# Branch hints for the matmul engine, chunk order inside the branches, and an earlier place for two blocks, in a two-layer transformer kernel

## The chip, the cores and the metric

One core of one Trainium2 chip. The metric is the device time of one execution in microseconds (us), the median over several runs. TensorE (PE) does matmuls (PEld is its weight load), VectorE is DVE, ScalarE ACT, GpSimd POOL; SyncE (SP) issues the transfers. Each engine runs its own instruction stream, branches included, and meets the others at semaphores.

## The reference, cut to what matters

256 tokens of width 1024 pass a first block (mLSTM and sparse attention, then a mixture of experts) and a second block (attention and a state-space branch). The change lies in the mixture of experts: each token goes to 4 of 32 experts; the grouping by expert depends on the data.

```python
logits = xf @ w_router + b_router
vals, idx = lax.top_k(logits, TOP_K);  gate = softmax(vals)
...
up = xb @ w_up[eb] + b_up[eb]            # [1024 x 2048] per expert
glu, lin = split(up, 2);  glu = min(glu, 7);  lin = clip(lin, -7, 7)
act = glu * sigmoid(1.702 * glu) * (lin + 1)
y = act @ w_down[eb] + b_down[eb]        # [1024 x 1024] per expert
```

After it the sum over experts is normalised (with the weight row `g_post_ffn`) and added to the residual.

## The kernel before, in words

**Weights.** All weights come through one stream of 1 MB transfers on SP's queue (class `Stream`, L159 to L189). In the expert part it owns 15 buffers of 1 MB; an expert needs 12 (8 of `w_up`, 4 of `w_down`). `ws.done(n)` gives a buffer back and issues the next transfer, in the order of the calls; SP waits there until the last reader of that buffer has finished. So a late reader holds back not only its buffer's successor but every transfer behind it.

**Loop (L2150 to L2200).** Step e computes expert e's up product and then expert e-1's down product. Tokens of an expert are split in chunks of 32 slots. The first chunk is always computed: for every fourth expert the token gather (tile `pga`), the bias (`up_bias`), 8 k-steps of matmuls into `pU` (one per 1 MB buffer), `swiglu`; then `down` into `pY`, a transpose `paT`, and `scatter` into `yacc`. How many tokens an expert has is known only at run time: `rv[e]` is loaded into registers of PE, ACT and DVE at k = 3 of step e (L2174).

**Branches.** `over_up(e)` (L2111) runs under `tc.If(rv[e] > 32)`: the second chunk into `pUo` and, nested in a second `tc.If(rv[e] > 64)`, the gather (`pgo`) and up product of the third chunk. `over_down(e-1)` (L2118) does the same for the down product, after the step's `scatter`. The body of such a branch is straight code; if the condition is false the engine jumps over it to a short arm in which it raises the semaphores that the body would have raised (EVENT_SEMAPHORE rows). In this input 13 experts have over 32 tokens, and two of them (11 and 25) over 64. The second chunk reads the same 8 (or 4) weight buffers as the first, and they are released after `over_up` (or `over_down`).

**After the loop.** L2202 to L2204: `far`, chunks 4 to 8 of every expert, all under one `tc.If(cmax > 96)` that PE, ACT, DVE and SP evaluate; here it is false, and the engines jump over it. Its weights would go to slots 3 and 4 of the pool `AR`. Then the last norm: squares of `yacc` into `jk` (L2213), `yg`, the reciprocal root, the residual, and block 2. The norm's weight row `gg2` is made in the loop's extra step e = 32 by `row_of` (8 transposes `prow`, two evictions), just before `over_down(31)`.

Of the kernel before, what the change touches and what calls it, by code (L numbers as in the profile page):

```python
# [7 lines left out]
F32 = mybir.dt.float32  # L8
# [5 lines left out]
OP = mybir.AluOpType  # L14
# [3 lines left out]
ET = mybir.EngineType  # L18
EPS = 1e-6

S, D = 256, 1024
# [134 lines left out]
NE = 32  # L156
# [189 lines left out]
def build(tc, A, out):  # L346
    nc = tc.nc
# [105 lines left out]
    def par(n):  # L453
        return cut(n, (PK, PK0, pk) if n in PK else (PK1, 0, [None, part.get("pk1")]))
# [64 lines left out]
    modc = con.tile([128, 48], F32, name="modc")  # L519
# [38 lines left out]
    def row_of(out, col, tiles, back=None):  # L558

        for j0 in range(0, 8, 4):  # L560
            t = yield from tiles(f"prow{j0}")
            for j in range(4):
                PE.transpose(t[:, 128 * j:128 * j + 128], col[:, j0 + j:j0 + j + 1].to_broadcast([128, 128]), ident)
            yield
            ev(out[:, 128 * j0:128 * j0 + 512], t)
            if back:
                back(f"prow{j0}")

    def at_once(f):
        def g(name):  # L570
            return f(name)
            yield
        return g
# [771 lines left out]
    t = PY("pmod")  # L1345
# [471 lines left out]
    t = []  # L1817
# [138 lines left out]
    rv = {}  # L1956
# [24 lines left out]
    def gates_lane():  # L1981

        pr, sm = sb.tile([128, 2, 4], F32, name="pr"), sb.tile([128, 2, 2], F32, name="sm")
        V.tensor_scalar(sm[:, :, 0:1], mx[:, :, 0:1], -1.0, None, op0=OP.mult)
        for i in range(2):
            ACT.activation(pr[:, i], mx[:, i, 0:4], AF.Exp, bias=sm[:, i, 0:1], accum_out=sm[:, i, 1:2])
        V.reciprocal(sm[:, :, 1:2], sm[:, :, 1:2])
        V.tensor_tensor(pr, pr, sm[:, :, 1:2].to_broadcast([128, 2, 4]), op=OP.mult)
        V.tensor_tensor(hit, hit, pr[:, :, :, None].to_broadcast(wide), op=OP.mult)
        V.tensor_reduce(gates, hit.rearrange("p i j e -> p i e j"), axis=AX.X, op=OP.add)  # L1990

        V.tensor_scalar(ghalf, gates, 0.5, None, op0=OP.mult)
        yield
        tg = PM("pgT")
        for i in range(2):
            PE.transpose(tg[:32, 128 * i:128 * i + 128], gates[:, i], ident)
        ACT.copy(gT, tg[:32, :256])
        yield
        for i in range(2):
            for n in range(2):  # L2000
                PE.matmul(yacc[i][n], gT[:, 128 * i:128 * i + 128], bd[:, 512 * n:512 * n + 512], start=True, stop=False,
                          skip_group_check=True)
        yield

    def up_bias(e, U):
        for q in range(4):
            PE.matmul(U[32 * q:32 * q + 32], e96[:, e:e + 1].to_broadcast([96, 32]),
                      bu3.rearrange("p (b c) -> p b c", b=2)[:, :, 256 * q:256 * q + 256], start=True, stop=False,
                      skip_group_check=True)
# [36 lines left out]
    def down(aT, wd):  # L2046

        t = PM("pY")
        for k in range(8):
            h, c = divmod(k, 2)  # L2050
            for q in range(4):
                PE.matmul(t[32 * q:32 * q + 32, 0:256], aT[:, c, 32 * h:32 * h + 32],
                          wd[k // 2][:, k % 2, 256 * q:256 * q + 256], start=k == 0, stop=k == 7, skip_group_check=True)
        return t
# [6 lines left out]
    def y_out(t, y):  # L2061
        for q in range(4):
            o, c = 32 * q, 256 * (q % 2)
            (ACT.copy if q % 2 else V.tensor_copy)(y[o:o + 32, c:c + 256], t[o:o + 32, 0:256])  # L2064
# [29 lines left out]
    def chunk_up(e, x, wu, act):  # L2094
        U = PO("pUo")
        up_bias(e, U)
        for k in range(8):
            up_k(U, x(k), k, wu(k))
        lc, th = (sb.tile([128, 256], F32, name=n, tag=n) for n in ("lco", "tho"))
        swiglu(U, act, lc, th)  # L2100

    def chunk_down(e, b, act, wd):
        gl_ = slots(e, 32 * b, "Go")
        next(gl_)
        a = sb.tile([128, 2, 128], F32, name="aTo", tag="aTo")
        act_T(act, a)
        g = next(gl_)
        y_out(down(a, wd), yz[2])
        scatter(g, yz[2])

    def over_up(e, wu, xT):  # L2111
        with tc.If(rv[e] > 32):  # L2112
            chunk_up(e, lambda k: xT[:, e % 4, k, 32:64], wu, ov[:, 2 * (e % 2)])
            with tc.If(rv[e] > 64):
                x = gather_chunk(e, 2)
                chunk_up(e, lambda k: x[:, k], wu, ov[:, 2 * (e % 2) + 1])

    def over_down(e, wd):  # L2118
        with tc.If(rv[e] > 32):
            chunk_down(e, 1, ov[:, 2 * (e % 2)], wd)  # L2120
            with tc.If(rv[e] > 64):
                chunk_down(e, 2, ov[:, 2 * (e % 2) + 1], wd)

    def far(e, r, b=3):

        with tc.If(r > 32 * b):
            x = gather_chunk(e, b)

            def weights(src, k):
                t = AR(3 + k % 2, "wf", [128, 2048])  # L2130
                v = t.rearrange("p (a b) -> p a b", a=src[0])
                SP.dma_start(v, src[2])
                return v

            lu, ld = block_loads(A["w_up"][e], 0, 2048, 1), block_loads(A["w_down"][e], 0, 1024, 2)
            chunk_up(e, lambda k: x[:, k], lambda k: weights(lu[k], k), ov[:, 4])
            wf = {}

            class Late:
                def __getitem__(self, k):  # L2140
                    if k not in wf:
                        wf[k] = weights(ld[k], k)
                    return wf[k]
            chunk_down(e, b, ov[:, 4], Late())
            if b < 7:
                far(e, r, b + 1)

    aT = {}
    gl = gates_lane()
    for e in range(NE + 1):  # L2150
        if e < NE:
            i0 = at[f"up{e}"][0]
            steps = iter(())
            if e % 4 == 0:
                xT = AR(0, "xT", [128, 4, 8, 64])
                steps = gather(xT, e, min(4, NE - e))
                next(steps)
            U = PU("pU")
            up_bias(e, U)
            act, lc, th = (sb.tile([128, 256], F32, name=n, tag=n, bufs=b) for n, b in (("act", 2), ("lc", 1), ("th", 1)))  # L2160
            if e:
                gs = slots(e - 1, 0, "G", 2)
                next(gs)
            wu = lambda k: ws.get(i0 + k)
            for k in range(8):
                if k % 2 == 0:
                    next(steps, None)
                up_k(U, xT[:, e % 4, k, 0:32], k, wu(k))
                if e == 0 and k < 3:
                    next(gl)  # L2170
                if e and k == 2:
                    g = next(gs)
                if k == 3:
                    rv[e] = nc.values_load(counts[0:1, e:e + 1], engines=(ET.PE, ET.Activation, ET.DVE), min_val=0, max_val=256)  # L2174
            swiglu(U, act, lc, th)
            over_up(e, wu, xT)
            for j in range(8):
                ws.done(i0 + j)
        if e:
            d0 = at[f"down{e - 1}"][0]  # L2180
            wd = [ws.get(d0 + k) for k in range(4)]
            if e == NE:
                gs = slots(e - 1, 0, "G", 2)
                next(gs)
                g = next(gs)
                gg2, ggc = AR(0, "gg2", [128, D]), sb.tile([128, 8], F32, name="ggc2")
                V.tensor_tensor(ggc, modc[:, 40:48], par("g_post_ffn"), op=OP.mult)
                for _ in row_of(gg2, ggc, at_once(PM)):
                    pass
                over_down(e - 1, wd)  # L2190
            y_out(down(aT[e - 1], wd), yz[e % 2])
        if e < NE:
            aT[e] = sb.tile([128, 2, 128], F32, name="aT", tag="aT", bufs=2)
            act_T(act, aT[e])
        if e:
            scatter(g, yz[e % 2])
            if e < NE:
                over_down(e - 1, wd)
            for k in range(4):
                ws.done(d0 + k)  # L2200
    many = (ET.PE, ET.Activation, ET.DVE, ET.SP)
    with tc.If(nc.values_load(cmax[0:1, 0:1], engines=many, min_val=0, max_val=256) > 96):  # L2202
        for e in range(NE):
            far(e, nc.values_load(counts[0:1, e:e + 1], engines=many, min_val=0, max_val=256))  # L2204

    sq, ss, rs = (sb.tile([128, n], F32, name=f"{m}3") for m, n in (("sq", 4), ("ss", 2), ("rs", 2)))
    yg = AR(8, "yg", [128, 2, D])
    jk = AR(7, "jk", [128, D])
    s3 = con.tile([128, 2], F32, name="ss4")
    for n in (1, 0):  # L2210
        for i in range(2):
# [37 lines left out]
```

## Time and profile before

| | |
|---|---|
| median of 3 runs | 1713.04 us (1710.18 to 1717.36) |
| the profiled execution's own time | 1716.04 us |
| its span, first to last instruction | 1714.2 us |
| mean granted TensorE clock | 0.935 |
| PE busy | 1424.8 us, 83% |
| bytes moved | 526 MB, 403 MB of them expert weights |

The expert part spans 254 to 1274 us of it. Times in rows are us from the span's start. A row of a timeline reads: start, length, engine, line, operation, tiles (out<-in), shape, count, and in brackets the idle time before it with what ended it. "PEq L2112" is PE's sequencer at a branch of that line, "issue" an idle time for which the profile shows no wait. Most operations are recorded by one helper and bear its line, L145; tiles tell them apart.

### The profile page before, as it was taken

The page shows a single profiled execution, that of the slowest core. Times are in us where ns is not written, and L with a number is a line of the kernel's source. Part 1 is how long each engine was busy: PE and PEld are TensorE (multiplying, and loading weights), DVE is VectorE, ACT ScalarE, POOL GpSimd, SP SyncE. Part 2 cuts the span into 40 slices and gives each one's busy share as a digit, 9 for nine tenths or more (in the row PEclk, how much of TensorE's full clock was granted, in tenths as well). Part 3 has the DMA queues.
Part 4 walks back from the last instruction along what each step waited for, and adds up shares of the span by engine and source line. Part 5 has one row for each costly group of instructions (what it writes and reads, how often), then busy time and mean ns, then how long its engine had stood idle before and what let it go on. Part 6 is the DMA issues. An engine that isn't in the chain of part 4 may idle for free. (4 is left out here: it accounts for less than half of the span.)

```text
span 1714.2 us, 28511 instructions
## 1 busy us (share of the span) xinstructions
PE 1424.8 (83%) x11403; PEld 845.3 (49%) x11403; DVE 661.5 (39%) x1508; ACT 435.9 (25%) x980; POOL 271.9 (16%) x387
## 2 busy tenths in 40 slices
PE   5999988887798898777766778887858888999998
PEld 2775652332233243232132233333227788999996
DVE  3556462121121122121111111221136798766767
ACT  3545331010010011010010010010025555654553
POOL 1127100000000000000000000000005652552533
PEclk8999999999899999889788988999988999999999
DMA  9746896999999988999999998999924344333452
GB/s 377 285 157 219 314 369 267 423 420 422 421 418 420 414 322 353 420 423 421 422 421 421 413 414 336 387 367 420 420 81 148 99 146 144 130 99 113 162 177 91
DMA packets 116487, 526.03 MB, mean 307 GB/s; under 512 B 8744, under 2 KB 11216, under 8 KB 80304
## 3 DMA queue, kind: packets, MB, share of 16 engines
q1 hardware_dynamic: 113392, 518.67, 76.0%
q10 hardware_dynamic: 2496, 3.92, 0.7%
q8 instruction: 157, 2.57, 0.6%
q0 software_dynamic: 384, 0.39, 0.1%
q14 instruction: 58, 0.48, 0.1%
HBM read 521.50 MB, written 1.06 MB: 305 GB/s over the span
## 5 line engine op out<-in xcount | busy, mean ns | idle before, releaser
L145 PE MATMUL pU<-w,xT 128*32 128x512 f32 x2048 | 266.2, 643 | 29.7 <-DMA w<-in_w_up 22.3
L145 PE MATMUL pg<-h,wH 128*128 128x256 f32 x1296 | 249.4, 292 | 9.8 <-ACT wH L254 3.1
L145 DVE TENSOR_TENSOR wL<-w,wH 128x512 fp32r<-128x512 f32 (+2 forms) x244 | 174.2, 728 | 111.1 <-PE pg L145 59.4
L145 PEld LDWEIGHTS pg<-h,wH 128*128 128x128 f32 x1296 | 205.5, 195 | 23.3 <-issue 7.0
L145 PE MATMUL pY<-w,aT 128*32 128x256 f32 x2048 | 151.2, 445 | 73.1 <-PEq L2112 41.3
L254 ACT CAST wH<-w 128x512 fp32r<-128x512 f32 (+4 forms) x312 | 176.1, 587 | 116.0 <-PE pg L145 101.7
L145 PE MATMUL pg<-h,wL 128*128 128x256 f32 (+1 forms) x648 | 186.2, 287 | 6.3 <-DVE wL L145 3.7
L145 POOL TENSOR_TENSOR xt<-yg,xt 128x512 f32<-128x512 f32 x1 | 1.5, 1485 | 1025.9 <-ACT yg L2219 1025.9
L145 PEld LDWEIGHTS pY<-w,aT 128*32 128x32 f32 x2048 | 79.3, 125 | 157.2 <-issue 74.8
L145 PEld LDWEIGHTS pU<-w,xT 128*32 128x32 f32 x2048 | 62.7, 115 | 171.9 <-issue 114.8
L145 DVE COPY yz<-pY 32x256 f32<-32x256 f32 x94 | 39.2, 417 | 248.6 <-PE pY L145 227.6
L145 PEld LDWEIGHTS pg<-h,wL 128*128 128x128 f32 (+1 forms) x648 | 125.7, 194 | 8.0 <-DVE wL L145 4.8
L145 POOL TENSOR_TENSOR wL<-w,wH 128x512 fp32r<-128x512 f32 (+2 forms) x68 | 87.8, 1297 | 222.6 <-PE pg L145 135.7
L2064 ACT COPY yz<-pY 32x256 f32<-32x256 f32 x94 | 34.1, 363 | 304.4 <-DVE yz L145 304.4
L145 PE MATMUL yacc<-yz,G 64*128 64x512 f32 x256 | 91.9, 627 | 17.8 <-ACT yz L2064 17.8
L2021 ACT ACTIVATE th<-act 128x256 f32<-128x256 f32 x32 | 13.3, 416 | 357.8 <-DVE act L145 357.8
L145 PE MATMUL pUo<-w,xT 128*32 128x512 f32 x832 | 92.1, 595 | 0.0
L145 DVE COPY G<-pG 128x256 f32<-128x256 f32 x32 | 13.6, 424 | 183.9 <-PE pG L145 183.9
L145 DVE TENSOR_SCALAR act<-pU 128x256 f32<-128x256 f32 x32 | 13.6, 424 | 155.5 <-PE pU L145 155.5
L145 PE MATMUL pg<-wH,h 128*128 128x512 f32 (+2 forms) x224 | 69.4, 393 | 3.6 <-ACT wH L254 1.9
L145 PE MATMUL pg<-yk,wH 128*128 128x256 f32 x384 | 68.6, 281 | 0.1
L145 PE MATMUL pY<-w,aTo 128*32 128x256 f32 x960 | 54.9, 380 | 9.1 <-DVE Go L145 8.5
(451 smaller groups left out, 1950.1 us busy)
## 6 DMA issues: line engine op xcount, KB each, us to landing
w<-in_w_up SPq DMA_DIRECT2D x256, 1024.0 KB, 17.3
w<-in_w_down SPq DMA_DIRECT2D x128, 1024.0 KB, 19.7
w<-in_w_in SPq DMA_DIRECT2D x48, 1024.0 KB, 4.9
w<-in_w_ada SPq DMA_DIRECT2D x24, 1024.0 KB, 8.5
w<-in_ada_w SPq DMA_DIRECT2D x12, 1024.0 KB, 6.7
w<-in_w_out SPq DMA_DIRECT2D x8, 1024.0 KB, 4.9
w<-in_w_branch_ssm SPq DMA_DIRECT2D x8, 1024.0 KB, 4.9
w<-in_w_branch_att SPq DMA_DIRECT2D x4, 1024.0 KB, 4.9
```

The costliest lines, as they stand in the source:

```text
L145: return f(*a, **k)
L254: self.nc.scalar.copy(H[:, a:b], p)
L2021: ACT.activation(th, act, AF.Tanh, scale=0.5 * 1.702)
L2064: (ACT.copy if q % 2 else V.tensor_copy)(y[o:o + 32, c:c + 256], t[o:o + 32, 0:256])
```

## The change

Four edits, all in the expert part. (1) `announce` marks, for PE only, a hint for the coming branch `up{e}` or `down{e}`, with the condition in a register; the mark for `up{e}` stands right after `up_bias`, that for `down{e-1}` ahead of `down` of the same step (for the last expert ahead of its step's releases). So the count is loaded one expert earlier. (2) Inside both branches the third chunk's `If` now stands ahead of the second chunk. (3) The far block moves from behind the loop to the start of step 31; its weights use slot 7. (4) `gg2` is made there too, in slot 7, and `jk` takes slot 0.

```diff
+    def announce(what, e):
+        tc.mark_branch_hint_location(f"{what}{e}", hint=rv[e] > 32, engines=hints)
...
     def over_up(e, wu, xT):
-        with tc.If(rv[e] > 32):
-            chunk_up(e, lambda k: xT[:, e % 4, k, 32:64], wu, ov[:, 2 * (e % 2)])
+        with tc.If(rv[e] > 32, label=f"up{e}"):
             with tc.If(rv[e] > 64):
                 x = gather_chunk(e, 2)
                 chunk_up(e, lambda k: x[:, k], wu, ov[:, 2 * (e % 2) + 1])
+            chunk_up(e, lambda k: xT[:, e % 4, k, 32:64], wu, ov[:, 2 * (e % 2)])
...
     def over_down(e, wd):
-        with tc.If(rv[e] > 32):
-            chunk_down(e, 1, ov[:, 2 * (e % 2)], wd)
+        with tc.If(rv[e] > 32, label=f"down{e}"):
             with tc.If(rv[e] > 64):
                 chunk_down(e, 2, ov[:, 2 * (e % 2) + 1], wd)
+            chunk_down(e, 1, ov[:, 2 * (e % 2)], wd)
...
-                t = AR(3 + k % 2, "wf", [128, 2048])
+                t = AR(7, "wf", [128, 2048])
...
+    rv[0] = counted(0)
     for e in range(NE + 1):
+        if e == NE - 1:
+            many = (ET.PE, ET.Activation, ET.DVE, ET.SP)
+            with tc.If(nc.values_load(cmax[0:1, 0:1], engines=many, min_val=0, max_val=256) > 96):
+                for o in range(NE):
+                    far(o, nc.values_load(counts[0:1, o:o + 1], engines=many, min_val=0, max_val=256))
+            gg2, ggc = AR(7, "gg2", [128, D]), sb.tile([128, 8], F32, name="ggc2")
+            V.tensor_tensor(ggc, modc[:, 40:48], par("g_post_ffn"), op=OP.mult)
+            for _ in row_of(gg2, ggc, at_once(PM)):
+                pass
...
             up_bias(e, U)
+            announce("up", e)
...
-                if k == 3:
-                    rv[e] = nc.values_load(counts[0:1, e:e + 1], engines=(ET.PE, ET.Activation, ET.DVE), min_val=0, max_val=256)
+                if k == 3 and e < NE - 1:
+                    rv[e + 1] = counted(e + 1)
             swiglu(U, act, lc, th)
             over_up(e, wu, xT)
+            if e == NE - 1:
+                announce("down", e)
...
                 over_down(e - 1, wd)
+            else:
+                announce("down", e - 1)
             y_out(down(aT[e - 1], wd), yz[e % 2])
```

The old places of the far block and of `gg2` are removed, and `jk = AR(7, ...)` becomes `jk = AR(0, ...)`.

## Rows read from the trace of the kernel before

**Rows 1.** Windows: stretch, length, busy PE PEld DVE ACT POOL, clock, DMA share, GB/s.

```profile
269.00:280.00 11.00, 10.43 (x101) 3.07 (x94) 2.46 (x7) 1.09 (x3) 0.00 (x0) 1.00 0.01 1
280.00:588.00 308.00, 252.28 (x2272) 99.82 (x2276) 59.76 (x153) 27.92 (x70) 0.00 (x0) 0.93 1.01 418
1028.00:1114.00 86.00, 72.62 (x660) 29.86 (x656) 16.44 (x45) 7.99 (x21) 0.00 (x0) 0.92 0.89 363
1114.00:1226.00 112.00, 91.59 (x812) 36.69 (x807) 20.86 (x53) 9.83 (x24) 0.00 (x0) 0.94 0.98 399
```

**Rows 2.** Waits of SP's queue: us in total, times, longest us.

```profile
SPq L180 <- PEq L2112: 131.7, 19, 12.5
SPq L180 <- PEq L2114: 129.6, 11, 26.2
```

**Rows 3.** Lines L2112, L2119, L2121, PE's branches: ns min/median/max, first and last start.

```profile
L2112 PEldq COMPARE_BRANCH  x32: 70/434/5938, 270.0 to 1225.0; - x32
...
L2119 PEldq COMPARE_BRANCH  x32: 65/414/6402, 299.7 to 1252.3; - x32
...
L2121 PEldq COMPARE_BRANCH  x26: 70/190/1507, 309.6 to 1263.2; - x26
```

**Rows 4.** Waits of PE, branch of L2112: us in total, times, longest.

```profile
PE pY L145 <- PEq L2112: 41.3, 17, 5.2
```

**Rows 5.** Timeline, PE and SP, expert 0's second chunk.

```profile
272.31 7.05 PE L145 MATMUL pUo<-w,xT 128*32 128x512 f32 x64
...
279.52 0.33 SPq L180 DMA_DIRECT2D w<-in_w_up  x1
```

**Rows 6.** Timeline of PE, expert 11's third chunk.

```profile
600.45 5.05 PE L145 MATMUL pgo<-So,xh 128*128 128x32 f32 x32 [2.22 <-DVE So L145]
...
605.91 8.78 PE L145 MATMUL pUo<-w,xo 128*32 128x512 f32 x64
```

**Rows 7.** Timeline of SP and PE, expert 25; time to landing from the page.

```profile
1007.99 2.54 SPq L180 DMA_DIRECT2D w<-in_w_up  x5
...
w<-in_w_up SPq DMA_DIRECT2D x256, 1024.0 KB, 17.3
...
1021.53 0.62 PE L145 MATMUL pU<-bu,e 96*32 96x512 bf16 x4 [4.27 <-PEq L2119]
1021.91 4.70 PE L145 MATMUL pU<-w,xT 128*32 128x512 f32 x24
```

**Rows 8.** Windows, the same columns, expert 25's first matmuls.

```profile
1021.00:1026.00 5.00, 4.46 (x24) 1.25 (x28) 0.00 (x0) 0.00 (x0) 0.00 (x0) 0.52 1.01 415
```

**Rows 9.** Timeline of PE, experts 26 to 31.

```profile
1066.24 4.48 PE L145 MATMUL pU<-w,xT 128*32 128x512 f32 x24 [3.50 <-DMA w<-in_w_down]
...
1125.15 2.05 PE L145 MATMUL pga<-S,xh 128*128 128x256 f32 x8 [4.38 <-PEq L2119]
...
1170.44 4.92 PE L145 MATMUL pY<-w,aT 128*32 128x256 f32 x44 [5.12 <-PEq L2112]
...
1189.99 2.75 PE L145 MATMUL pU<-w,xT 128*32 128x512 f32 x24
...
1213.01 0.40 PE L145 MATMUL pU<-bu,e 96*32 96x512 bf16 x4
...
1225.02 1.07 PE L145 MATMUL pU<-w,xT 128*32 128x512 f32 x8 [1.57 <-DMA w<-in_w_up]
```

**Rows 10.** Line L2202, the far block's branch on PE.

```profile
L2202 PEldq COMPARE_BRANCH  x1: 3726/3726/3726, 1269.5 to 1269.5; - x1
```

**Rows 11.** Timeline of PE and ACT, step 32 and the norm's start.

```profile
1252.26 1.06 PE L145 MATMUL prow<-cst__67,ggc 128*128 128x128 f32 x8 [0.68 <-DVE ggc L145]
1253.55 0.44 PE L145 MATMUL paT<-cst__67,ov 128*128 128x128 f32 x2 [0.24 <-ACT gg L515]
...
1268.20 2.83 PE L145 MATMUL yacc<-yz,G 64*128 64x512 f32 x8 [0.97 <-ACT yz L2064]
...
1273.40 0.60 ACT L2213 ACTIVATE jk<-yacc 128x512 f32<-128x512 f32 x1 [4.40 <-PEq L2202]
```

More of the change, by code (lines that the diff above doesn't have):

```diff
@@ L2109, in chunk_down @@
         scatter(g, yz[2])
+    hints = (ET.PE,)
+    def announce(what, e):
+        tc.mark_branch_hint_location(f"{what}{e}", hint=rv[e] > 32, engines=hints)
     def over_up(e, wu, xT):
-        with tc.If(rv[e] > 32):
-            chunk_up(e, lambda k: xT[:, e % 4, k, 32:64], wu, ov[:, 2 * (e % 2)])
+        with tc.If(rv[e] > 32, label=f"up{e}"):
             with tc.If(rv[e] > 64):
@@ L2149, in build @@
     gl = gates_lane()
+    counted = lambda e: nc.values_load(counts[0:1, e:e + 1], engines=(ET.PE, ET.Activation, ET.DVE), min_val=0, max_val=256)
+    rv[0] = counted(0)
     for e in range(NE + 1):
+        if e == NE - 1:
[7 more added lines that the diff above has]
+                pass
         if e < NE:
@@ L2185, in build @@
                 g = next(gs)
[L2186 to L2189, printed above, removed]
                 over_down(e - 1, wd)
+            else:
+                announce("down", e - 1)
             y_out(down(aT[e - 1], wd), yz[e % 2])
@@ L2200, in build @@
                 ws.done(d0 + k)
[L2201 to L2204, printed above, removed]
     sq, ss, rs = (sb.tile([128, n], F32, name=f"{m}3") for m, n in (("sq", 4), ("ss", 2), ("rs", 2)))
     yg = AR(8, "yg", [128, 2, D])
-    jk = AR(7, "jk", [128, D])
+    jk = AR(0, "jk", [128, D])
     s3 = con.tile([128, 2], F32, name="ss4")
```

## The prediction

> **What bounds the kernel now.** I read the windows by stage first, then the waits of SP and PE, then the single lines and the timeline. In the expert part the bound is mostly the weight stream: from 280 to 588 us the transfers are busy all the time at 418 GB/s, while PE is busy 252 of 308 us [rows 1]. At that pace a 1 MB buffer takes 2.5 us. A shorter PE therefore gains only where the stream goes unfed. That is so at the start (share 0.01 from 269 to 280) and behind experts 11 and 25, which have a third chunk (0.89 from 1028 to 1114, against 0.98 after it) [rows 1]. SP, when it waits for a buffer, waits most for PE's arrival behind a branch: 131.7 us at L2112 and 129.6 us at L2114, 11 times [rows 2].
>
> Two different things hide in these rows. At L2114 it is bookkeeping: the inner branch stands last, so with no third chunk all 8 buffers come free only in its empty arm, after the whole second chunk. At L2112 and L2119 it is the jump itself. A branch that is entered costs PE 0.07 us; one that is jumped costs up to 5.9 and 6.4 us [rows 3], and PE's matmuls behind L2112 waited 41.3 us for it [rows 4]. The inner jump at L2121, over a shorter body, never took over 1.5 us [rows 3]. So the cost hangs on how far the jump goes: code that is not there yet has to be fetched.
>
> **Part 1, the order of the chunks.** Expert 0 shows what a second chunk costs the stream. Its matmuls run from 272.31 for 7.05 us, and the first transfer after them is issued at 279.52 [rows 5]. With the inner branch ahead, PE first makes that short jump (I take 0.5 us, an estimate between the median of 0.19 and the worst of 1.5 [rows 3]); the first buffer is then free after an eighth of 7.05 us, so at 273.7, and one more every 0.9 us, faster than transfers take them. The stream restarts 5.6 us earlier; I take **-5.0**. As the stream is busy without a break until 588, this arrives there whole. The other ten such experts gain the same on paper, but there the queue still holds several transfers, and early buffers are worth nothing.
>
> Experts 11 and 25 pay for it. Before, the chunk that releases the buffers was the third one, and PE's 2.22 us wait for DVE's mask stood behind the second [rows 6]. Now the gather comes straight after the first chunk, where DVE is still in `swiglu` (about 2.9 us, an estimate from those 2.22 and the branches ahead of it), then the gather's 5.05, the third chunk's 9.3 with its bias, about 1.0 until DVE has emptied the single `pUo` buffer, then 1.2 to the first release: 19.4 us after the first chunk. Before it was 7.3 + 2.2 + 5.05 + 0.5 + 1.7 (the first k-step at the pace of [rows 6]) = 16.7. So the first buffer comes **+2.7** later, and PE is busy **+1.8** longer. After expert 11 other gains (the down buffers of expert 10, released early; a jump at expert 12) cancel this; I take 0 there.
>
> **Part 2, the hints.** A jump's price is more than its idle time. [...] The last `w_up` buffer of expert 25 was issued by 1010.1 and landed some 17.3 us later [rows 7], at 1027.4, so its first chunk could have ended at 1028.3; it ended near 1031.3 (1021.91 + 4.70, then 40 matmuls at the pace of expert 30 and a small transpose). With the jump at 0.4 us: **-3.0** (bounds 0 and -6.2). The same jump at expert 26 (4.38 us, and slow gather matmuls behind it [rows 9]) gives about **-6** on PE's chain. The one at expert 29 (5.12) I count at 0: by then the stream is the later of the two (below); its bound is -4.6. The marks are two more register steps and a marker on PE's sequencer, 64 times in all. PE's sequencer runs ahead of its matmuls (L2112's branch is executed before the matmuls ahead of it are done), and the stream covers the rest: 0; without that cover at most 0.1 to 0.2 us each (the entered branch's 0.07 and the inner jump's 0.19 are the nearest rows), some 2 us from expert 25 on. The counts' loads only move by one step: 0.
>
> **Part 3, the far block and the norm's row.** At the end two things go. The row of `gg2` holds PE from 1251.58 to 1253.55: **-2.0** [rows 11]. The far jump makes ACT start the norm at 1273.40, although the last `scatter` ended at 1271.03 [rows 11]: **-2.2**, leaving 0.15 for the semaphore. In step 31 they come back: the jump 3.7 us [rows 10] (transfers were idle then; 6.1, as the long ones of [rows 3], is likelier under load), the row 2.0, and slow first matmuls 2.0: 7.7 to 10.1, I take 10. ACT and DVE jump too, beside PE, and SP, which has up to eight transfers queued. The cover: expert 31's first chunk ran from 1213.01 to 1226.1, 13.1 us against 7.7 for one that waits for nothing (bias 0.4, 64 matmuls at 2.75 per 24), since it waited for its weights (the last wait, 1.57 us [rows 9]). So 5.3 of the 10 are hidden: **+4.7**.
>
> **The sum.** On PE's chain: -5.0 - 3.0 + 1.8 - 6.0 = -12.2 by expert 28. On the stream: -5.0 - 3.0 + 2.7 = -5.3 at expert 25's first release. Of what it goes unfed later (11% of 86 us is 9.5, of which expert 25 itself about 6; 2% of 112 is 2.2 [rows 1]) I let 4 go, through earlier releases: -9.3. The later counts: -9.3 into step 31, + 4.7 = -4.6 at the end of its first chunk, from where PE bounds until the norm; - 2.0 - 2.2 gives -8.8. Block 2 only shifts. The profiled execution took 1716.04 us, so 1707.2; it lies 3.0 above the median of the runs, so against that median I forecast **1704.2**.
>
> **The rivals.** *The hints do nothing* (never taken up, or the fetch is still late). Then PE's chain has -5.0 + 1.8 = -3.2, the stream about -4.3; -3.2 + 4.7 - 4.2 = -2.7, 1710.3. For it: nothing in this trace shows a hint at work. Against: between mark and branch lie over 100 PE instructions, 7 us or more, and the longest jump is 6.4.
>
> *The hinted code pushes out the code that comes next*, and the kernel is slower. The trace has such stalls in straight code: at expert 26 PE stood 3.50 us within a chunk (the transfer it is put down to is no match: that chunk reads `w_up`), and the next 24 matmuls took 4.48 [rows 9]: 5.2 us in all. From expert 25 on six hinted jumps are taken (up and down of 26, 27, 29). PE's chain without them stands at -12.2 + 4.7 - 4.2 = -11.7, so it decides from the third stall on; with four, +9.1, 1722. Against it: the inner jumps, right behind an entered branch, find their code. [...]
>
> *More goes than I count*: expert 26's straight-code stall is gone because the code lies differently, and the far jump costs 3.7. Then the stream has -12, the far block +2.7, the end -4.2: -13.5, 1699.5.
>
> *The inner jump misses*, now that it comes early in the body. Six second chunks of experts 28 to 31 depend on it; two misses of 3 us take 6 back, 1710.
>
> **How the numbers follow.** Forecast 0.45 (half of it beyond 0.5%, as it lies on that line), hints without effect 0.20, more than counted 0.17, pushed-out code 0.10, inner misses 0.08. 0.5% of the median is 8.6 us, about what a measurement of this kernel can tell from no change: faster 0.41, same 0.47, slower 0.12. The range takes the bounds of expert 29's jump and of the far block below, and reaches up to where three stalls stand: 1692 to 1719.
>
> **What would show it.** PE's longest branch at L2112 and L2119 under 1 us (else the hints fail); expert 0's first reissue near 274; expert 25's first reissue 19 to 20 us after its first chunk; the far branch ahead of expert 31's matmuls with 6 to 10 us of PE idle; ACT's `jk` right behind the last `scatter`. New "issue" stalls of 2 to 4 us would make the forecast wrong upwards, a stream without gaps behind expert 25 downwards.

## The result, and the profile after: 1.1% slower

The changed kernel took a median of 1732.66 us (1730.75 to 1734.33, 4 runs) against 1712.4 for the kernel before beside it (1710.18 to 1717.36, 4 runs): a ratio of 1.011, 95% interval 1.0089 to 1.013. The forecast was 1704.2, faster or the same. The profiled execution took 1730.75 us, its span is 1729.0 (before 1714.2).

Windows of the changed kernel, with the columns of [rows 1]; the last stretch is new.

```profile
269.00:280.00 11.00, 9.02 (x84) 2.36 (x80) 1.61 (x4) 0.42 (x1) 0.00 (x0) 0.96 0.32 102
280.00:588.00 308.00, 255.96 (x2313) 94.30 (x2305) 62.18 (x160) 28.36 (x71) 0.00 (x0) 0.93 1.02 421
1028.00:1114.00 86.00, 72.02 (x672) 31.48 (x672) 15.84 (x44) 7.58 (x20) 0.00 (x0) 0.92 0.87 354
1211.00:1246.00 35.00, 15.17 (x86) 5.07 (x86) 2.16 (x7) 1.32 (x3) 0.00 (x0) 0.71 0.72 292
```

The start did fill (share 0.32 where it was 0.01 [rows 1]). Behind expert 25 nothing improved (0.87, before 0.89). The loss sits in the last line: from 1211 to 1246 us PE is busy 15.17 of 35 us, and the granted clock there is 0.71, so part of its work goes by at a lower clock, 0.55 from 1239.9 to 1243.0 (the last 40 matmuls of the chunk take 5.83 us; at the pace of expert 30 [rows 9] they would take 4.58). Expert 30's first chunk still ends at 1197.15 (before 1197.54); expert 31's ends at 1245.80 (before 1226.08, 19.7 earlier). The last norm starts 14.9 us later than before [rows 11], and the span is 14.8 longer. So the difference between these two executions arises in one step of the loop: step 31 loses 20.1 us, and 4.8 come back before the norm.

Timeline of that step, PE, DVE and ACT:

```profile
1210.84 2.83 PE L145 MATMUL yacc<-yz,G 64*128 64x512 f32 x8 [0.57 <-ACT yz L2064]
...
1221.26 1.94 PE L145 MATMUL prow<-cst__67,ggc 128*128 128x128 f32 x8 [7.58 <-PEq L2161]
...
1223.53 3.80 PE L145 MATMUL pU<-w,xT 128*32 128x512 f32 x24
...
1238.24 0.59 ACT L515 COPY gg<-prow 128x512 f32<-128x512 f32 x1 [26.21 <-SPq L2161]
1238.29 0.69 DVE L145 COPY gg<-prow 128x512 f32<-128x512 f32 x1 [20.45 <-SPq L2161]
1238.90 0.59 DVE L145 TENSOR_SCALAR gt<-cst__68,pos,ghalf 128x128 f32<-128x128 f32 x2
1239.35 0.38 PEld L145 LDWEIGHTS pG<-cst__67,gt 128*128 128x128 f32 x2 [12.93 <-ACT gg L515]
1239.38 0.66 PE L145 MATMUL pG<-cst__67,gt 128*128 128x128 f32 x2 [12.05 <-DVE gt L145]
...
1239.97 5.83 PE L145 MATMUL pU<-w,xT 128*32 128x512 f32 x40
```

Read it from below. PE's `pG` waits 12.05 us for DVE's `gt`; DVE stands ahead of `gt` in the eviction of the norm's row into `gg2`; and that eviction waits, as ACT's does, for SP's sequencer at the far block's branch (L2161). The row's matmuls were done at 1223.2, so the row lay 15 us in PSUM. The source view of that branch says what SP did (operation, count, duration in ns, first and last start):

```profile
L2161 SPq EVENT_SEMAPHORE  x9: 17/17/17, 1228.9 to 1238.1; - x9
L2161 DVEq EVENT_SEMAPHORE  x2: 21/21/21, 1217.4 to 1217.6; - x2
L2161 ACTq EVENT_SEMAPHORE  x2: 17/17/17, 1218.3 to 1218.4; - x2
L2161 PEldq EVENT_SEMAPHORE  x2: 51/51/51, 1220.8 to 1221.0; - x2
...
L2161 PEldq COMPARE_BRANCH  x1: 6451/6451/6451, 1214.3 to 1214.3; - x1
...
L2161 SPq COMPARE_BRANCH  x1: 50/50/50, 1223.8 to 1223.8; - x1
```

PE, DVE and ACT raise two semaphores each in the short arm and are through at 1221. SP has nine. It reaches the branch at 1223.8; its own jump takes 5.0 us, to 1228.9. The fifth to the eighth semaphore go at 1230.62, 1233.09, 1235.57 and 1238.05, each 0.01 to 0.02 us behind the landing of a transfer of the weight stream (1230.60, 1233.08, 1235.56, 1238.04), and the ninth goes right after. Eight of the nine are the semaphores that the stream's transfers raise in turn: in the arm SP waits for each of them and then raises it, in place of the far block's transfers. So SP goes through its empty arm no faster than the transfers it has already issued land. `gg2` lies in slot 7, the slot the change gave to the far block's weights, and in the trace both evictions of the row wait for these same eight semaphores. From 1217.75 to 1249.18, 31 us, SP issued no transfer either.

A second loss is spread over the whole expert part. The wait for DVE's inner branch (L2119) did not exist before:

```profile
L2119 DVEq EVENT_SEMAPHORE  x11: 21/21/21, 274.3 to 1247.8; - x11
...
  PE pUo L145: 22.3, 11
```

In all 11 experts with a second but no third chunk, PE's second chunk waits 2.0 us (22.3 in all) for DVE's empty inner arm. `pUo` is one PSUM buffer. With the third chunk's `If` ahead, that arm is what releases it, and DVE gets there only after the `swiglu` of the first chunk. Expert 0, and expert 28, where the chunk itself also went slower:

```profile
274.39 0.40 PE L145 MATMUL pUo<-bu,e 96*32 96x512 bf16 x4 [1.98 <-DVEq L2119]
274.62 7.04 PE L145 MATMUL pUo<-w,xT 128*32 128x512 f32 x64
...
1139.05 0.40 PE L145 MATMUL pUo<-bu,e 96*32 96x512 bf16 x4 [2.03 <-DVEq L2119]
1139.27 1.02 PE L145 MATMUL pUo<-w,xT 128*32 128x512 f32 x3
1140.71 8.11 PE L145 MATMUL pUo<-w,xT 128*32 128x512 f32 x59 [0.41 <-issue]
```

The granted clock was 1.00 in the 10 us ahead of this and is 0.84 in the 11 us from 1139. Over all second chunks the page's mean of one such matmul rose from 595 to 640 ns.

The jumps did get shorter. Branches of the two outer `If`s on PE, minimum, median and maximum in ns (before: [rows 3]):

```profile
L2118 PEldq COMPARE_BRANCH  x45: 77/191/4712, 269.4 to 1252.4; - x45
L2125 PEldq COMPARE_BRANCH  x45: 70/290/6245, 297.0 to 1279.7; - x45
```

Added over the 38 that are jumped, they take 74.4 us instead of 130.1, and 19 of them take under 0.5 us (10 before). Some still cost the full price. At the end, the first square of `yacc` follows the last `scatter` (1286.29, 2.83 long) at once, no longer a far jump:

```profile
1288.30 0.60 ACT L2227 ACTIVATE jk<-yacc 128x512 f32<-128x512 f32 x1 [1.21 <-PE yacc L145]
```

### The profile page after: what moved, and what is told of

Its sections match the earlier page's. It is cut to its first block, busy times and chain, and to the rows that moved or that the text cites. A ratio compares the mean times of both kernels' runs of the same rounds, so it can differ in the third digit from the quotient of the medians.

```text
span 1729.0 us, 28678 instructions
## 1 busy us (share of the span) xinstructions
PE 1431.3 (83%) x11403; PEld 831.5 (48%) x11403; DVE 662.2 (38%) x1508; ACT 436.0 (25%) x980; POOL 272.2 (16%) x387
## 5 line engine op out<-in xcount | busy, mean ns | idle before, releaser
L145 PE MATMUL pY<-w,aT 128*32 128x256 f32 x2048 | 140.7, 418 | 53.2 <-DMA w<-in_w_down 31.2
L145 PEld LDWEIGHTS pU<-w,xT 128*32 128x32 f32 x2048 | 57.7, 114 | 185.3 <-issue 100.1
L145 PEld LDWEIGHTS pY<-w,aT 128*32 128x32 f32 x2048 | 68.8, 117 | 137.7 <-DMA w<-in_w_down 42.6
L145 PE MATMUL yacc<-yz,G 64*128 64x512 f32 x256 | 98.2, 687 | 16.8 <-ACT yz L2064 16.8
L145 PE MATMUL pUo<-w,xT 128*32 128x512 f32 x832 | 101.7, 640 | 0.4 <-issue 0.4
L145 DVE TENSOR_SCALAR act<-pU 128x256 f32<-128x256 f32 x32 | 13.6, 425 | 180.8 <-PE pU L145 180.8
L145 DVE COPY G<-pG 128x256 f32<-128x256 f32 x32 | 13.6, 425 | 151.3 <-PE pG L145 151.3
## 6 DMA issues: line engine op xcount, KB each, us to landing
w<-in_w_down SPq DMA_DIRECT2D x128, 1024.0 KB, 19.7
```

Source lines behind the costliest of these rows:

```text
L145: return f(*a, **k)
```

## The experiments

Every ratio is against runs of the kernel before on the same chip in the same session. Its medians there were 1714.09 (experiments 1 to 4), 1715.16 (5 to 8) and 1713.68 (9 to 12).

### Experiments 1 to 4: which part of the change loses

**1.** The changed kernel with the far block and the row back at their old places.

```diff
-                t = AR(7, "wf", [128, 2048])
+                t = AR(3 + k % 2, "wf", [128, 2048])
...
-        if e == NE - 1:
-            many = (ET.PE, ET.Activation, ET.DVE, ET.SP)
...
-            gg2, ggc = AR(7, "gg2", [128, D]), sb.tile([128, 8], F32, name="ggc2")
...
                 g = next(gs)
+                gg2, ggc = AR(0, "gg2", [128, D]), sb.tile([128, 8], F32, name="ggc2")
...
+    many = (ET.PE, ET.Activation, ET.DVE, ET.SP)
+    with tc.If(nc.values_load(cmax[0:1, 0:1], engines=many, min_val=0, max_val=256) > 96):
...
-    jk = AR(0, "jk", [128, D])
+    jk = AR(7, "jk", [128, D])
```

> Hints and the new chunk order, with the far block and the norm's row back at their old places. Theory (the far block's move is the whole loss: SP's arm of that branch waits for the transfers in flight, and the row's evictions wait for SP): expert 30 ends its first chunk in the changed kernel 0.4 us before the old one, so without the move the time is that of the kernel before, 1712 give or take 4 us, and the first chunk of expert 31 ends near 1226 us instead of 1245.8. Rival (hints push out code, or the second chunk's 2.03 us wait for DVE costs it): at least half of the 20 us stays, 1722 or more.

Measured: 1716.15 (1709.51 to 1721.95, 12 runs), ratio 1.0016 (1.0001 to 1.003). Expert 31's first chunk ends at 1224.98 (before 1226.08).

**2.** The kernel before with these two moved and nothing else.

```diff
-                t = AR(3 + k % 2, "wf", [128, 2048])
+                t = AR(7, "wf", [128, 2048])
...
+        if e == NE - 1:
+            many = (ET.PE, ET.Activation, ET.DVE, ET.SP)
...
+            gg2, ggc = AR(7, "gg2", [128, D]), sb.tile([128, 8], F32, name="ggc2")
...
```

> The kernel before with only the far block and the norm's row moved (slots as in the change). Theory: +20 us, 1732, with the same 12 us wait of expert 31's transpose for DVE and SP's semaphores of the empty arm spread over the landings of the transfers in flight. Rival (hints or order are at fault): within 5 us of 1712, as 10 us come back in step 31 and 4 us go at the end.

Measured: 1731.97 (1731.16 to 1734.56, 6 runs), ratio 1.011 (1.0091 to 1.0129). That is the loss of the whole change. Its step 31 shows the same chain, without hints or new order:

```profile
1238.97 0.69 DVE L145 COPY gg<-prow 128x512 f32<-128x512 f32 x1 [26.21 <-SPq L2153]
...
1240.06 0.66 PE L145 MATMUL pG<-cst__67,gt 128*128 128x128 f32 x2 [18.67 <-DVE gt L145]
```

**3.** The hints alone (the old order of the chunks, all else at its old place).

```diff
+        with tc.If(rv[e] > 32, label=f"up{e}"):
...
+        with tc.If(rv[e] > 32, label=f"down{e}"):
...
+            announce("up", e)
...
+                announce("down", e - 1)
```

> The kernel before with only the hints. Theory: a hinted jump is short where the mark ran 10 us or more ahead of it and stays long where it ran 5 to 8 us ahead; up to 5 us faster, 1707 to 1712. Rival (pushed-out code): new idle times of 2 to 4 us in straight code, 1717 or more.

Measured: 1709.55 (1707.76 to 1713.24, 12 runs), ratio 0.998 (0.9967 to 0.9993). A gain of 0.2%: the 38 jumps take 72.4 us in place of 130.1, but of those 58 us only 4.5 show in the median. That the stream hides the rest is likely by [rows 1], but no run shows it.

**4.** The order alone.

```diff
-            chunk_up(e, lambda k: xT[:, e % 4, k, 32:64], wu, ov[:, 2 * (e % 2)])
             with tc.If(rv[e] > 64):
                 x = gather_chunk(e, 2)
                 chunk_up(e, lambda k: x[:, k], wu, ov[:, 2 * (e % 2) + 1])
+            chunk_up(e, lambda k: xT[:, e % 4, k, 32:64], wu, ov[:, 2 * (e % 2)])
...
-            chunk_down(e, 1, ov[:, 2 * (e % 2)], wd)
             with tc.If(rv[e] > 64):
                 chunk_down(e, 2, ov[:, 2 * (e % 2) + 1], wd)
+            chunk_down(e, 1, ov[:, 2 * (e % 2)], wd)
```

> The kernel before with only the new chunk order. Theory: the stream restarts 4 to 5 us earlier at expert 0, but each of the 13 second chunks now begins 2.0 us later, because its bias waits until DVE has passed the empty inner arm, and PE's clock falls in some: 1710 to 1716. Rival (early release is worth its 5 us to the end): 1707 or less.

Measured: 1717.0 (1708.87 to 1729.75, 12 runs), ratio 1.0029 (1.0007 to 1.0051): the order alone makes the kernel slower. The 2 us waits are there without hints:

```profile
  PE pUo L145: 22.3, 11
```

The four fit together. The move of far block and row is the 1.1%, the hints bring 0.2%, and the order, which I had as a gain, costs 0.3%.

### Experiments 5 to 8: which mechanism

**5.** The order alone, with the third chunk's product in a buffer of another PSUM pool.

```diff
-    def chunk_up(e, x, wu, act):
-        U = PO("pUo")
+    def chunk_up(e, x, wu, act, P=PO):
+        U = P("pUo")
...
-                chunk_up(e, lambda k: x[:, k], wu, ov[:, 2 * (e % 2) + 1])
+                chunk_up(e, lambda k: x[:, k], wu, ov[:, 2 * (e % 2) + 1], PM)
```

> The new order alone, with the third chunk's up product in a PSUM buffer of pool PM instead of the one buffer that the second chunk needs. Theory: the order alone lost its gain because in each of 11 experts the second chunk's bias waited 2.03 us (22.3 us in all) for DVE's empty inner arm, and because the slower first matmuls behind that wait made some chunks 8.9 to 9.6 us instead of 7.27. Without that wait no row of PE waiting for DVE at the inner up branch is left, all second chunks but the two of experts 11 and 25 take 7.3 us, and the early start of the stream stays: 1709 to 1713 against 1717 with the wait. Rival: the order loses at experts 11 and 25, whose buffers come free later, or through jumps that now fall at worse moments; then the wait goes and the time stays at 1715.5 to 1718.5.

Measured: 1711.2 (1702.87 to 1715.63, 12 runs), ratio 0.9976 (0.996 to 0.9992). One PSUM buffer turns the order from 0.29% slower to 0.24% faster. Expert 0 now starts its second chunk 0.47 us after the first, behind the inner jump, as the prediction had it:

```profile
271.14 0.40 PE L145 MATMUL pUo<-bu,e 96*32 96x512 bf16 x4 [0.47 <-PEq L2113]
271.35 7.05 PE L145 MATMUL pUo<-w,xT 128*32 128x512 f32 x64
```

PE's wait for DVE there is gone, as expected. But three of the 13 second chunks still took 7.4, 8.2 and 9.9 us in place of 7.27 (one was slow before, three in experiment 4, five in the changed kernel), so the wait is not the only cause of a slow chunk. And though this kernel has no hint, its 38 jumps took 95.5 us in place of 130.1, 17 of them under 0.5 us: the price of a jump changes with more than the hints.

**6.** The far block moved, the row left in the last step.

```diff
-                t = AR(3 + k % 2, "wf", [128, 2048])
+                t = AR(7, "wf", [128, 2048])
...
+        if e == NE - 1:
+            many = (ET.PE, ET.Activation, ET.DVE, ET.SP)
+            with tc.If(nc.values_load(cmax[0:1, 0:1], engines=many, min_val=0, max_val=256) > 96):
...
```

> The kernel before with the far block alone moved to step 31; the norm's row stays in the last step, in slot 0. Theory: in step 31 SP's empty arm holds its semaphores until the transfers in flight have landed (to about 1238), but PE, ACT and DVE lose only by the row in slot 7, which waits for that arm. With the row elsewhere expert 31's first chunk ends no more than 5 us later than before (about 1231 at most, not 1246), SP issues nothing for 15 to 20 us all the same, and as one transfer alone stands behind it in the expert part, the time is 1713 to 1719. Rival: the drain of SP itself or PE's jump over the far block costs the 18 us; then the first chunk of expert 31 ends near 1246 again and the time is 1728 to 1733.

Measured: 1711.73 (1707.38 to 1714.38, 10 runs), ratio 0.9984 (0.9971 to 0.9997). This is the run that decides. SP drains just as in the changed kernel, and nobody loses 18 us by it; the time is even a little under what I gave:

```profile
L2153 SPq EVENT_SEMAPHORE  x9: 17/17/17, 1228.6 to 1238.0; - x9
...
L2153 PEldq COMPARE_BRANCH  x1: 6055/6055/6055, 1208.3 to 1208.3; - x1
...
  PE pU L145: 7.0, 1
```

```profile
1214.63 0.62 PE L145 MATMUL pU<-bu,e 96*32 96x512 bf16 x4 [6.97 <-PEq L2153]
1215.01 4.22 PE L145 MATMUL pU<-w,xT 128*32 128x512 f32 x24
```

SP issued nothing from 1217.8 to 1238.1, but only one transfer of the expert part (the last `w_down` buffer) stood behind. PE's wait for the far jump is 6.97 us, and expert 31's first chunk ends at 1224.03, 2.0 before the old kernel's, where expert 30's was 5.2 ahead: the far block cost 3.2 us in step 31. It gave back more at the end: `jk` starts 5.8 us earlier than before.

**7.** The row moved alone.

```diff
+        if e == NE - 1:
+            gg2, ggc = AR(7, "gg2", [128, D]), sb.tile([128, 8], F32, name="ggc2")
...
-                gg2, ggc = AR(0, "gg2", [128, D]), sb.tile([128, 8], F32, name="ggc2")
...
-    jk = AR(7, "jk", [128, D])
+    jk = AR(0, "jk", [128, D])
```

> The kernel before with the norm's row alone moved to step 31 (slot 7, jk in slot 0); the far block stays behind the loop. Theory: the row leaves the end, where it held PE for 2.0 us, and in step 31 it lies beside PE's wait for expert 31's weights: 1711 to 1713 against 1714. Rival: the evictions of the row delay ACT and DVE in step 31 as much as it held PE at the end, or the first matmuls of the chunk fall to the lower clock: no change, 1714 to 1716. By either, nothing of the 18 us is seen.

Measured: 1712.55 (1707.2 to 1717.79, 12 runs), ratio 0.9991 (0.9977 to 1.0005). The row in slot 7 is harmless when the far block isn't there; the interval takes in no change as well as the 2.0 us I gave the row, so its own gain stays open.

**8.** Hints, the row in step 31, and the far block behind the loop with a hint of its own.

```diff
                 over_down(e - 1, wd)
+                cm = nc.values_load(cmax[0:1, 0:1], engines=many, min_val=0, max_val=256)
+                tc.mark_branch_hint_location("far", hint=cm > 96, engines=hints)
...
+    with tc.If(cm > 96, label="far"):
```

> Hints in the old order, the norm's row moved to step 31, and the far block at its old place but with a hint of its own, marked behind the last down branch. Theory: the hints bring 4 us as they did alone (1709.5), the row 2.0, and the hinted far jump 2.2 (PE's jump falls from 3.7 to about 0.4 us, and the first square of yacc follows the last scatter within 0.3 us): 1704 to 1707, the fastest of all. Rival: the mark for the far block lies too near its branch (down product and scatter of the last expert, about 8 us) and the jump keeps its price: 1707 to 1709.

Measured: 1708.82 (1706.98 to 1712.88, 8 runs), ratio 0.9967 (0.9953 to 0.9981), 0.1% better than the hints alone, which the two intervals leave unproven. In the profile the far jump fell from 3.73 us to 0.46, with its mark 5.7 us ahead, but ACT has no mark, its own jump still takes 3.0 us (1262.0 to 1265.0), and `jk` starts 0.75 us behind the last `scatter`, so 1.6 of the 2.2 are gained. The time lies where the rival put it, but not for its reason: the mark was not too near. The gains I had added up were too large by 2 us or more.

### Experiments 9 to 12: the change mended

**9.** The changed kernel, with the row in rows 4 to 7 of `ov` instead of slot 7. Row 4 is not quite unused, as the expectation has it: the far block would put its product there. But DVE writes that and PE reads it; no transfer of SP's touches it.

```diff
-            gg2, ggc = AR(7, "gg2", [128, D]), sb.tile([128, 8], F32, name="ggc2")
+            gg2, ggc = ov[:, 4:8].rearrange("p a b -> p (a b)"), sb.tile([128, 8], F32, name="ggc2")
```

> The changed kernel with one thing different: the norm's row lies in four unused rows of the tile ov instead of slot 7, so its evictions have nothing to do with the slot of the far block's weights. Theory: the 18 us are the wait of these two evictions for SP's empty arm. Then SP still holds its semaphores to about 1238 and issues nothing for 15 to 20 us, but ACT and DVE evict the row at once, the first chunk of expert 31 ends 15 us or more earlier than in the changed kernel (1245.8), near 1228, and the time is 1711 to 1716 against 1732.7. Rival: with the hints and the new order the drained queue itself is what PE waits for; then 1724 or more.

Measured: 1719.09 (1717.49 to 1721.11, 6 runs), ratio 1.0037 (1.0023 to 1.005). 13.6 us under the changed kernel by the medians, 12.5 by the two ratios, and the mechanism is as expected: SP's semaphores still go to 1240.0, the row is evicted as soon as it is there,

```profile
L2161 SPq EVENT_SEMAPHORE  x9: 17/17/17, 1230.8 to 1240.0; - x9
...
1224.67 1.94 PE L145 MATMUL prow<-cst__67,ggc 128*128 128x128 f32 x8 [7.74 <-PEq L2161]
1225.79 0.59 ACT L515 COPY ov<-prow 128x512 f32<-128x512 f32 x1 [10.50 <-PE prow L145]
...
1226.64 0.69 DVE L145 COPY ov<-prow 128x512 f32<-128x512 f32 x1 [5.46 <-PE prow L145]
```

but expert 31's first chunk ends at 1235.4, not 1228, and the time is 3 us above what I gave it. PE came to step 31 late. From expert 28's first chunk to expert 29's took 33.2 us: the bias wait, a chunk of 8.97 us, then a full jump, 4.56 us of it idle, and a first chunk that took 10.4 us instead of 7.8:

```profile
1141.30 0.40 PE L145 MATMUL pUo<-bu,e 96*32 96x512 bf16 x4 [2.03 <-DVEq L2119]
...
1162.02 0.62 PE L145 MATMUL pU<-bu,e 96*32 96x512 bf16 x4 [4.56 <-PEq L2125]
```

**10.** Both mends: the row in `ov` and the PSUM buffer of experiment 5.

```diff
...
-                chunk_up(e, lambda k: x[:, k], wu, ov[:, 2 * (e % 2) + 1])
+                chunk_up(e, lambda k: x[:, k], wu, ov[:, 2 * (e % 2) + 1], PM)
...
-            gg2, ggc = AR(7, "gg2", [128, D]), sb.tile([128, 8], F32, name="ggc2")
+            gg2, ggc = ov[:, 4:8].rearrange("p a b -> p (a b)"), sb.tile([128, 8], F32, name="ggc2")
```

> The changed kernel with both mends: the row in ov, and the third chunk's up product in its own PSUM buffer. Theory: the two faults add up and nothing else is wrong with the change, so the mended PSUM buffer gives another 4 to 6 us, as it did in the order alone: 1706 to 1711, faster than before by 0.2 to 0.5%. Rival: with the hints in place the jumps fall at worse moments once PE is earlier, and the second mend gives nothing on top: 1711 to 1716.

Measured: 1706.53 (1699.75 to 1708.93, 8 runs), ratio 0.9954 (0.9936 to 0.9972). The same stretch takes 22.9 us. The bias wait is gone, the chunk takes 7.27, and the jump behind it is short this time:

```profile
1140.72 0.40 PE L145 MATMUL pUo<-bu,e 96*32 96x512 bf16 x4 [0.18 <-PEq L2119]
1140.94 7.05 PE L145 MATMUL pUo<-w,xT 128*32 128x512 f32 x64
...
1155.66 0.40 PE L145 MATMUL pU<-bu,e 96*32 96x512 bf16 x4 [0.46 <-PEq L2125]
```

So the PSUM buffer was worth 12.6 us here (1719.09 to 1706.53) where I expected 4 to 6. Of the 10.3 us in this stretch 1.9 are the wait, 1.7 and 2.6 are the slower matmuls of the two chunks, and 4.1 are a jump that was short this time; why that one changed was not tried.

**11.** Experiments 5 and 8 together: hints, the order with its own PSUM buffer, the row moved, the far block behind the loop with its hint. Against experiment 8 (`chunk_up` as in experiment 5, `over_down` as in experiment 4):

```diff
...
-            chunk_up(e, lambda k: xT[:, e % 4, k, 32:64], wu, ov[:, 2 * (e % 2)])
             with tc.If(rv[e] > 64):
                 x = gather_chunk(e, 2)
-                chunk_up(e, lambda k: x[:, k], wu, ov[:, 2 * (e % 2) + 1])
+                chunk_up(e, lambda k: x[:, k], wu, ov[:, 2 * (e % 2) + 1], PM)
+            chunk_up(e, lambda k: xT[:, e % 4, k, 32:64], wu, ov[:, 2 * (e % 2)])
...
```

> Hints, the new order with the third chunk's own PSUM buffer, the row moved to step 31 in slot 7, and the far block behind the loop with a hint of its own. Theory: the parts are independent, the order's 4 us come on top of the 6 us of hints, row and far hint together: 1702 to 1706, the fastest of all. Rival: hints and order gain at the same places (the stream can be early only once), and the time stays at 1706 to 1709.

Measured: 1703.52 (1701.9 to 1706.64, 5 runs), ratio 0.9944 (0.9929 to 0.9959): the lowest median of all (its interval overlaps that of experiment 10), 0.56% under the kernel before and, by the two ratios, 1.6% under the changed one. Its last norm starts at 1262.80, 10.6 us earlier than before:

```profile
1262.80 0.60 ACT L2229 ACTIVATE jk<-yacc 128x512 f32<-128x512 f32 x1 [3.58 <-ACTq L2218]
```

**12.** Hints alone, with the mark for `down` right behind the one for `up`.

```diff
             announce("up", e)
+            if e:
+                announce("down", e - 1)
...
-            else:
-                announce("down", e - 1)
```

> Hints alone in the old order, but the mark for the down branch stands right behind that for the up branch, so that it leads its branch by 15 us and more instead of 5 to 12. Theory: a hinted jump is cheap when the fetch had about 10 us; if two marks can be open at once, the longest down jump falls from 6.2 to under 1 us while the up jumps stay as they are: 1706 to 1709 against 1709.5 with the marks apart. Rival: the second mark takes the place of the first; then the up jumps cost 3 to 6 us again, as without marks, the down jumps are cheap, and the time is 1710 to 1714.

Measured: 1713.11 (1708.73 to 1715.56, 12 runs), ratio 0.9994 (0.9982 to 1.0007). The gain of the hints is not seen, though the intervals of the two ratios overlap. The up jumps take 55.4 us in all (37.8 with the marks apart in experiment 3 and 40.3 in experiment 8, 67.1 without marks), and PE's `pY` waited 30.7 us for them instead of 15.3. The down jumps hardly change (33.4 against 34.5), although their mark now stands 16 us and more ahead, and four of the 19 still took 5.8 to 6.2 us. So the rival held in its time and in the up jumps, not in the down jumps. That the second mark spoils the first is the likely reading, from one execution of each; up and down together, 88.7 us, are no more than in experiment 8 with the marks apart (90.5). A longer lead by itself does not make a jump cheap.

## Why the prediction was wrong

**Part 3, the far block: the step that failed.** I wrote that "ACT and DVE jump too, beside PE, and SP, which has up to eight transfers queued", and priced PE's jump alone. SP's part in the branch got no term, though the sentence names its queue. Two things were missing: how long SP stays at the branch with transfers in flight (14.3 us, 1223.8 to 1238.1: 5.0 for its own jump, the rest for landings), and who waits for it. The second is what costs: both the far block's weights and the row went to slot 7, so the row's evictions waited for SP, DVE's `gt` waited behind them, and PE behind `gt`. Experiments 6, 7 and 9 separate the two. The drain without the shared slot costs no 18 us (1711.73), the row in slot 7 without the far block costs nothing (1712.55), and the row elsewhere takes 12.5 to 13.6 us off the changed kernel. What is queued behind each added wait on its own engine I worked out for PE only.

The terms I did price were near. The far jump took 6.45 us (6.1 expected), the net cost in step 31 without the clash was 3.2 us in experiment 6 (4.7 expected, the row included). For the slow first matmuls I took 2.0, from expert 25's 1.95; expert 31's 24 took 1.05 us above 2.75 here and 1.47 in experiment 6 (3.80 and 4.22). At the end the first chunk of expert 31 is followed by `jk` after 42.5 us instead of 47.3: 4.8 gained, 4.2 expected.

**Part 1, the order: wrong sign.** The gain at the start came, 3.9 of 5.0 us: the first reissue follows expert 0's first chunk by 3.3 us instead of 7.2 (275.72 against 272.41; before [rows 5]). The ten others, where I put zero, lost: 22.3 us of waits for DVE's empty inner arm, 2 of them at expert 0 and 20 there. The mechanism was in my own text, "DVE is still in `swiglu`", and in the 2.22 us of [rows 6], but I applied it only to experts 11 and 25, where the third chunk is computed, and not where it is skipped. A skipped body is also a writer of `pUo`, and its release comes in DVE's order. At experts 11 and 25 themselves the first reissue came 20.0 and 21.5 us after the first chunk (19.4 expected).

**Part 2, the hints: right in kind, smaller in effect.** Alone they bring 0.2% (experiment 3), about 4 us. In its profile PE's chain is 10.1 us ahead at expert 28 and 8.4 at expert 31, 2.0 of which it already had at the end of expert 0's first chunk; I had 9.0 from the jumps at experts 25 and 26. At expert 25 itself the gain was 1.3 us of the 3.0 (25.9 us from expert 24's first chunk to the end of its own, before 27.3). The bound of 6.2 there is the 4.27 us of idle time and the 1.95 us that the first 24 matmuls took above those of expert 30 (4.70 [rows 7], 2.75 [rows 9]), at a granted clock of 0.52 [rows 8]. That PE's longest branch would be "under 1 us" did not come true: 6.2 us remain. I took it that a mark stands 7 us or more ahead and that this suffices, since the longest jump is 6.4. Neither held. In the changed kernel 10 of the 38 marks stand less than 7 us ahead of their branch, the nearest 5.6. And in experiment 3, 18 of the 38 jumps take under 0.5 us and 13 over 2 us, these with leads from 4.9 to 13.8 us. How much of the shortening is the hints' own stays open, since experiment 5 has shorter jumps without any.

**The rivals.** That the hints do nothing is ruled out narrowly, by the 0.9967 to 0.9993 of experiment 3. That hinted code pushes out the code that comes next, with 1722 the nearest of my times to the result, was right in sign by accident: experiment 2 has the whole loss without a hint. Its "issue" stalls are not settled. PE's `pU` and `pY` waited 22.1 us for "issue" before, 28.4 with the hints alone (experiment 3) and 7.8 in the changed kernel; here are the two rows of each, in this order.

```profile
PE pY L145 <- issue: 14.1, 8, 3.2
PE pU L145 <- issue: 8.0, 5, 4.1
...
PE pY L145 <- issue: 17.5, 8, 3.5
PE pU L145 <- issue: 10.9, 5, 2.9
...
PE pY L145 <- issue: 4.6, 5, 3.0
PE pU L145 <- issue: 3.2, 2, 1.9
```

So hints alone went with 6 us more of such stalls, and experiment 3 was still faster than the kernel before. These runs neither bear this rival out nor exclude it. What the traces do show is that a long jump ends behind a transfer of code. The page of the kernel before has a queue for it (packets, MB, share):

```profile
q8 instruction: 157, 2.57, 0.6%
```

There each of PE's 26 outer jumps over 1 us ended 1.3 to 1.6 us behind the end of one of these packets of 16 KB (1.4 to 1.5 at the 17 of the changed kernel), and during the 12 shorter ones, all under 0.7 us, none was under way. Why 10 of the 38 took under 0.5 us before, with no mark, no run shows. That the inner jump misses was not it either, though it took up to 2.6 us. Without the far block and row, hints and order as they stood gave 1716.15 (experiment 1), inside the range given; the two missing waits together put the result 13.7 us above its upper end.

## What to carry to other kernels

An `If` that was not taken still had its place in the order of each engine that evaluates it: the empty arm released the body's buffer only when DVE got there (PE waited 2.0 us for it at each of 11 second chunks), and SP, which issues transfers, stood there 14.3 us, until those in flight had landed. So before moving such a block, list for each engine of it what it still has to do at the new place, and give no tile that is needed soon a buffer or slot which the skipped body writes from an engine that gets there late. Here another buffer cured the wait for a skipped body twice, one in PSUM and one for the row (1.1% slower to 0.5% faster).

## What the runs showed of the hardware that was not expected

SP's empty arm went at the pace of the transfers in flight, 2.47 us for each of the last semaphores; behind the loop the same nine lie within 0.6 us (1260.8 to 1261.4 in experiment 11). The jump over the far block is not PE's alone: it took SP 5.0 us too. Behind a branch hint many jumps took 0.3 to 0.5 us and others about 6: in the changed kernel leads of 5.6 us gave 0.4 and 6.1 us. But both kinds occur without a hint as well, 10 of 38 under 0.5 us before and 17 in experiment 5. With two marks open at once the up jumps took 55.4 us, against 37.8 and 40.3 with one. Why one jump is short and the next is not stays open.
